# The first two blocks of rows multiplied with raw tokens, and the norm and the shift applied to the sums

## The chip, the cores and the metric

The kernel runs on one core of a Trainium2 chip. The metric is the device time of one execution in microseconds. A core has TensorE (PE in the profile, its weight loads PEld), VectorE (DVE), ScalarE (ACT), GpSimd (POOL) and SyncE (SP), which run side by side and wait for one another by semaphores. SBUF is the memory that they work from, PSUM the one that PE writes its sums to, and DMAs bring data from HBM.

## The reference

One layer of a block for 512 latent tokens of width 2048, with 256 context tokens. What matters here is its beginning:

```
shift, scale, gate = jnp.split(silu(c) @ w_ada + b_ada, 3)
h = rmsnorm(x, norm_g) * (1 + scale) + shift
p = h @ w_in                                # 512 x 2048 by 2048 x 9216
q, k, v, z_a, u_b, z_b, g_a, g_b = columns of p
attn = attention(rope(rmsnorm(q)), [k, kc], [v, vc])
y = (sig(g_a) * ((attn * silu(z_a)) @ w_pa)
     + sig(g_b) * ((fourier(u_b) * silu(z_b)) @ w_pb)) @ w_o
out = rmsnorm(x + gate * y, final_g)
```

`rmsnorm(x, g)` is x times a factor per token, 1/sqrt(mean(x^2) + eps), times g. So a row of h is, for input channel k and token t, x[k,t] * gain[k] * r[t] + shift[k], where gain is norm_g * (1 + scale). All is float32.

## The kernel before

The tokens lie transposed in SBUF: `xt` holds 16 blocks of 128 channels by 512 tokens. A block of rows of h (512 tokens, 128 channels) is made from `xt`, the gain and shift of its channels and the factor `rx` of each token (`make_h`, lines 378 to 383), and split in two parts, `hh` (rounded to fp32r) and `hl` (what is left). Weights are split likewise into `whi` and `wlo` (`split_from`, lines 119 to 121: ACT rounds, DVE subtracts). A product of float32 accuracy is then three products on PE (`mm3`, lines 219 to 223).

The start has these parts, in the program's order:

- The token loads (`XCH`, lines 64 and 336), then the modulation matrix of block 0 (two loads of 1 MB, `wada_load`), three start pieces of the weights, and the matrix of block 1 (lines 373 to 376), all on SP's queue. From block 2 on, the matrix comes by POOL's queue into four buffers.
- `squares` (lines 351 to 371): the tokens' squares by ACT, three of 16 by DVE, pairs added by DVE, and eight products on PE with a matrix of ones, which sum over the channels and leave the sum of each token on all partitions; root and reciprocal give `rx`.
- `modulation` of a block (lines 447 to 455): silu(c) times its part of the matrix (32 PE instructions, line 391), a copy by ACT, two transposes (line 401), and three small DVE operations that give shift and gain. For block 0, some products with ones that nothing uses keep PE at work (`warm`, line 411).
- The loop over blocks (lines 464 to 476): modulation, rows, then as many of the start's products as are owed.

`start_work` (lines 413 to 445) is a generator of these products: for each group of blocks (`GROUPS`, line 40) ten column tiles of 128 (four for the Fourier branch, four for its gate, two for heads of q) whose sums are added up over the groups in `part` and `q01` (`pt`, `keep`), and four tiles of V (`vals`). Its PSUM sums come from a ring of four banks (`bank`). A group of one block has 10 x 3 + 4 x 3 = 42 products of 128 x 128 by 512 columns. The weights of a piece are loaded ahead into four raw buffers on SP's queue (`start_load`, `load_more`) and split three pieces ahead (`get`). The loads wait for the buffers.

Each engine works through its instructions in a fixed order. The programming layer sets it when the kernel is built: by the order of the program, but an instruction whose inputs are estimated to be late lets later ones pass.

## Time and profile before

| | us |
|---|---|
| median of 3 runs | 1391.73 |
| lowest and highest | 1391.26, 1393.59 |
| the profiled execution | 1392.62 |
| its span, first to last instruction | 1390.8 |
| PE busy, share of the span | 1358.8, 98% |
| DVE busy | 890.4, 64% |
| ACT busy | 617.8, 44% |

The profile is of one execution. A row of its groups or of its timeline names the line, the engine, the operation and the tile that is written from those that are read, with shapes as partitions by elements. A group's row ends with its count, its busy time in us, the mean of one in ns, and, behind the bar, how long the engine had stood idle before and for whom. In the timeline a row starts with start and length in us from the first instruction, and shows in brackets an idle time before it. In the chain of waits a row is start, length and what the chain ran through there. A matmul's length in the profile is longer than its distance to the next, since they overlap; the distance is what counts.

### The profile page before, as it was taken

How to read it: one execution, taken by the hardware profiler on the slowest of the kernel's cores; microseconds unless marked ns; L12 is line 12 of the kernel's file. 1: busy time of each engine (PE TensorE's matmuls, PEld its weight loads, DVE VectorE, ACT ScalarE, POOL GpSimd, SP SyncE). 2: the span in 40 equal slices, each digit the busy share in tenths (PEclk: the TensorE clock that was granted, in tenths of full speed). 3: DMA queues.
4: the chain of work that ended last, by engine and by line, in shares of the span. 5: the costliest groups of instructions: out<-in, count | busy, mean ns of one | idle time of the engine just before them, and what ended most of it. 6: DMA issues, size and time to landing. Idle time of an engine off the chain costs nothing.

```text
span 1390.8 us, 17626 instructions
## 1 busy us (share of the span) xinstructions
PE 1358.8 (98%) x6858; PEld 1113.7 (80%) x6858; DVE 890.4 (64%) x1172; ACT 617.8 (44%) x849; POOL 106.6 (8%) x161
## 2 busy tenths in 40 slices
PE   7999999999999999999999899999999999999996
PEld 4667789888888888888888688888888888888874
DVE  5765596867866668666644776665856544437767
ACT  5322253534545544544544645444544322233534
POOL 0110000011100001000001100000010100000100
PEclk9999999999999999999999999999999999999998
DMA  9897453545543435434447998988898844244883
GB/s 384 328 349 264 159 185 107 185 123 184 162 140 107 128 112 160 139 99 121 135 131 275 312 285 239 259 227 257 266 269 301 327 151 137 76 137 153 182 224 136
DMA packets 73812, 275.29 MB, mean 198 GB/s; under 512 B 8448, under 2 KB 9088, under 8 KB 69376
## 3 DMA queue, kind: packets, MB, share of 16 engines
q1 hardware_dynamic: 52272, 183.18, 39.8%
q0 software_dynamic: 16272, 73.42, 18.7%
q10 hardware_dynamic: 5184, 17.57, 3.3%
q8 instruction: 54, 0.88, 0.3%
q14 instruction: 30, 0.25, 0.1%
HBM read 248.95 MB, written 25.17 MB: 197 GB/s over the span
## 4 chain that ended last, share of the span: by engine, by line
PE 89%; DMA 5%; DVE 4%; ACT 1%; issue 1%; DVEq 0%; SPq 0%; ACTq 0%
PE pb L221 12%; PE pb L222 12%; PE pb L223 12%; PE x L222 7%; PE x L223 7%; PE x L221 6%; PE y L222 6%; PE y L223 6%; PE y L221 6%; PE pd L221 3%; PE pd L223 3%; PE pd L222 3%; PE pd L930 2%; PE pd L391 2%; DMA wr<-in_w_g 2%; DVE wlo L121 1%
## 5 line engine op out<-in xcount | busy, mean ns | idle before, releaser
L120 ACT ACTIVATE whi<-wr 128x1024 fp32r<-128x1024 f32 x188 | 195.7, 1045 | 336.5 <-PE y L223 89.5
L121 DVE TENSOR_TENSOR wlo<-wr,whi 128x1024 fp32r<-128x1024 f32 x188 | 225.8, 1204 | 170.9 <-ACT whi L120 170.5
L221 PE MATMUL pb<-hh,whi 128*128 128x512 f32 x512 | 206.7, 405 | 1.3 <-ACT hh L381 1.3
L222 PE MATMUL pb<-hl,whi 128*128 128x512 f32 x512 | 200.7, 392 | 0.1
L223 PE MATMUL pb<-hh,wlo 128*128 128x512 f32 x512 | 200.4, 392 | 0.0
L222 PE MATMUL y<-wlo,s 128*128 128x512 f32 x348 | 137.1, 394 | 7.1 <-DVE wlo L121 7.1
L221 PE MATMUL y<-whi,s 128*128 128x512 f32 x348 | 136.6, 393 | 0.6 <-ACT whi L120 0.6
L223 PE MATMUL y<-whi,s 128*128 128x512 f32 x348 | 136.3, 392 | 0.0
L221 PEld LDWEIGHTS pb<-hh,whi 128*128 128x128 f32 x512 | 96.1, 188 | 22.5 <-issue 3.7
L223 PEld LDWEIGHTS pb<-hh,wlo 128*128 128x128 f32 x512 | 96.1, 188 | 21.0 <-issue 0.4
L222 PEld LDWEIGHTS pb<-hl,whi 128*128 128x128 f32 x512 | 96.4, 188 | 17.1 <-DVE hl L382 1.0
L222 PE MATMUL x<-wlo,s 128*128 128x512 f32 x248 | 97.0, 391 | 0.6 <-DVE wlo L121 0.6
L221 PE MATMUL x<-whi,s 128*128 128x512 f32 x248 | 97.0, 391 | 0.0
L223 PE MATMUL x<-whi,s 128*128 128x512 f32 x248 | 96.8, 390 | 0.0
L120 ACT ACTIVATE whi<-R 128x1024 fp32r<-128x1024 f32 x57 | 60.0, 1058 | 55.7 <-PE x L223 38.0
L222 PEld LDWEIGHTS y<-wlo,s 128*128 128x128 f32 x348 | 65.6, 189 | 23.3 <-DVE wlo L121 9.8
L121 DVE TENSOR_TENSOR wlo<-R,whi 128x1024 fp32r<-128x1024 f32 x57 | 69.0, 1220 | 20.4 <-ACT whi L120 20.4
L921 ACT ACTIVATE p<-pd,mx 128x768 f32<-128x768 f32 x48 | 43.2, 900 | 84.5 <-DVE mx L919 84.5
L221 PEld LDWEIGHTS y<-whi,s 128*128 128x128 f32 x348 | 65.8, 189 | 14.8 <-ACT whi L120 1.0
L223 PEld LDWEIGHTS y<-whi,s 128*128 128x128 f32 x348 | 65.8, 189 | 13.6
L121 DVE TENSOR_TENSOR ptl<-pd,pth 128x768 fp32r<-128x768 f32 x48 | 45.8, 953 | 33.0 <-ACT pth L120 33.0
L221 PE MATMUL pb<-whi,hh 128*128 128x512 f32 x144 | 57.1, 397 | 0.0
(283 smaller groups left out, 2705.1 us busy)
## 6 DMA issues: line engine op xcount, KB each, us to landing
wr<-in_w_g SPq DMA_DIRECT2D x80, 512.0 KB, 8.0
wa<-in_w_ss POOLq DMA_DIRECT2D x28, 1024.0 KB, 8.5
wr<-in_w_m SPq DMA_DIRECT2D x44, 512.0 KB, 3.7
wr<-in_w_gate SPq DMA_DIRECT2D x32, 512.0 KB, 3.7
wr<-in_w_pab SPq DMA_DIRECT2D x32, 512.0 KB, 5.2
R<-in_w_g POOLq DMA_DIRECT2D x32, 512.0 KB, 10.1
wr<-in_w_o SPq DMA_DIRECT2D x32, 512.0 KB, 4.1
wr<-in_w_start SPq DMA_DIRECT2D x26, 512.0 KB, 7.1
```

The costliest lines, as they stand in the source:

```text
L120: nc.scalar.activation(hi, src, ACT.Copy)
L121: nc.vector.tensor_tensor(lo, src, hi.bitcast(F32), op=ALU.subtract)
L221: nc.tensor.matmul(o, ah, bh, start=start, stop=False, skip_group_check=cont)
L222: nc.tensor.matmul(o, ah, bl, start=False, stop=False, skip_group_check=cont)
L223: nc.tensor.matmul(o, al, bh, start=False, stop=stop, skip_group_check=cont)
L391: nc.tensor.matmul(acc[32 * j : 32 * j + 32, :256], c2[:, kk, :], w[:, k, :], start=kk < 4, stop=kk >= KK - 4)
L921: nc.scalar.activation(p, sc[:, :NKEY], ACT.Exp, bias=mx[:, 0:1], accum_out=mx[:, 1:2])
L930: nc.tensor.transpose(tp[:, k * P : (k + 1) * P], p[:, k * P : (k + 1) * P], ident)
```

## The change

Block by block, h @ w is sum over k of (x * gain * r + shift) * w. For the first two blocks the change multiplies x * gain (`make_early`) instead of the rows of h, sums as before, and adds w's product with the shift (`sft`, two equal columns; its sums are gathered in `sv`). When `rx` is there the ten sums of 128 x 512 are multiplied by it on DVE, and the shift's sums are added with the next group (`keep`). V's tiles have tokens on the partitions; for them the true rows of the two blocks are made later, and the two blocks' V pieces become one. The order of loads on SP is: matrix of block 0, tokens of block 0, two start pieces, matrix of block 1, tokens of block 1, two start pieces, the other tokens. The norm is computed after the two blocks' modulation: squares are added on DVE into one running sum, and PE sums them per token with the squares as weights (`token_norm`), so that the root and the reciprocal work on four columns; a diagonal matrix and one product with ones bring the factors back to all partitions. It stands in the program after 45 of the 60 products of the two blocks.

```diff
--- before.py
+++ after.py
@@ -38,6 +38,8 @@
 NS = len(START)
 
 GROUPS = [(0, 1), (1, 1), (2, 2), (4, 4), (8, 4), (12, 4)]
+
+EARLY = 2
 RAW = 4
 
 HL, MORE_HL = 3, 2
@@ -61,7 +63,7 @@
     f = {"P1": "Z5", "P2": "S2", "Q6": "S3", "P7": "S4"}.get(name)
     return [(f, pc - 1)] if f and g == 0 and pc in (1, 2) else []
 
-XCH = [(0, 2), (2, 2), (4, 4), (8, 4), (12, 2), (14, 2)]
+XCH = [(0, 1), (1, 1), (2, 2), (4, 4), (8, 4), (12, 2), (14, 2)]
 
 
 def start_pieces():
@@ -71,7 +73,10 @@
     for kb, nk in GROUPS:
         per = 8 // nk
         new = [(kb, nk, t, min(per, NS - t)) for t in range(0, NS, per)]
-        new += [(kb + i, min(2, nk), -1, 4) for i in range(0, nk, 2)]
+        if kb + nk == EARLY:
+            new.append((0, EARLY, -1, 4))
+        elif kb >= EARLY:
+            new += [(kb + i, min(2, nk), -1, 4) for i in range(0, nk, 2)]
         for p in new:
             cols = p[1] * p[3] * P
             r.append((off, cols) + p)
@@ -333,47 +338,49 @@
         (nc.gpsimd if kb > 1 else nc.sync).dma_start(w, w_ss[kb, :, 8 * h : 8 * h + 8, :])
         return w
 
-    for a, n in XCH:
+    def x_load(i):
+        a, n = XCH[i]
         nc.sync.dma_start(xt[:, a : a + n, :], xT[:, a : a + n, :])
+
+    wada = {(0, h): wada_load(0, h) for h in range(2)}
+    x_load(0)
+    for _ in range(2):
+        start_load()
+    wada.update({(1, h): wada_load(1, h) for h in range(2)})
+    x_load(1)
+    for _ in range(2):
+        start_load()
+    for i in range(2, len(XCH)):
+        x_load(i)
 
 
     c2 = pap.tile([P, KK, 32], F32, name="c2")
     nc.vector.memset(c2, 0.0)
     rt = pap.tile([P, 1], F32, name="rt")
+    ex = pap.tile([P, 2 * KK], F32, name="ex")
     ce = pap.tile([P, 2 * KK], F32, name="ce")
-    nc.scalar.activation(ce, cvt, ACT.Exp, scale=-1.0)
-    nc.scalar.activation(rt, ce[:, 0:1], ACT.Sqrt)
-    nc.vector.tensor_scalar(ce, ce, 1.0, None, op0=ALU.add)
+    nc.scalar.activation(ex, cvt, ACT.Exp, scale=-1.0)
+    nc.scalar.activation(rt, ex[:, 0:1], ACT.Sqrt)
+    nc.vector.tensor_scalar(ce, ex, 1.0, None, op0=ALU.add)
     nc.vector.reciprocal(ce, ce)
     nc.vector.tensor_tensor(c2[:, :, 0:2].rearrange("p k j -> p j k"),
                             cvt.rearrange("p (j k) -> p j k", j=2),
                             ce.rearrange("p (j k) -> p j k", j=2), op=ALU.mult)
-    def squares(srcs, n, r, new, run=None):
+    def squares(srcs, n, r, new, run):
 
         acc = bank2()
         for q in range(0, KK, 2):
             a, b = new(), new()
             for t, src in zip((a, b), srcs(q)):
-                if run is None and t is b and q in (4, 8, 10):
-                    nc.vector.tensor_tensor(t, src, src, op=ALU.mult)
-                else:
-                    nc.scalar.activation(t, src, ACT.Square)
+                nc.scalar.activation(t, src, ACT.Square)
             nc.vector.tensor_tensor(a, a, b, op=ALU.add)
-            if run is None:
-                nc.tensor.matmul(acc[:, :n], ones, a, start=q == 0, stop=q == KK - 2)
-            elif q == 0:
+            if q == 0:
                 nc.vector.tensor_copy(run, a)
             else:
                 nc.vector.tensor_tensor(run, run, a, op=ALU.add)
-        if run is not None:
-            nc.tensor.matmul(acc[:, :n], ones, run, start=True, stop=True)
+        nc.tensor.matmul(acc[:, :n], ones, run, start=True, stop=True)
         nc.scalar.activation(r, acc[:, :n], ACT.Sqrt, bias=eps_t[:, 0:1], scale=1.0 / D)
         nc.vector.reciprocal(r, r)
-
-    wada = {(0, h): wada_load(0, h) for h in range(2)}
-    while todo and len(ahead) < 3:
-        start_load()
-    wada.update({(1, h): wada_load(1, h) for h in range(2)})
 
     def make_h(hi, lo, src, rr, kb, j, pool, n):
         tmp = pool.tile([P, n], F32, tag="htmp", bufs=2, name=uid("ht"))
@@ -414,13 +421,15 @@
         ends = {kb + nk for kb, nk in GROUPS}
         begins = {kb for kb, nk in GROUPS}
 
-        def keep(dst, acc, first):
+        def keep(dst, acc, first, add=None):
             if first:
                 nc.scalar.copy(dst, acc)
+            elif add is not None:
+                nc.vector.scalar_tensor_tensor(dst, acc, add, dst, op0=ALU.add, op1=ALU.add)
             else:
                 nc.vector.tensor_tensor(dst, acc, dst, op=ALU.add)
 
-        vacc = None
+        vacc, sacc = None, None
         for p in start_pieces():
             kb, nk, t, nt = p[2:]
             wh, wl = get(("start", p))
@@ -429,9 +438,22 @@
                     acc = bank()
                     c = slice(P * i, P * i + P)
                     for k in range(nk):
-                        mm3(acc, wh[:, k, c], wl[:, k, c], hhi[kb + k], hlo[kb + k], k == 0, k == nk - 1)
-                    keep(pt(t + i), acc, kb == 0)
+                        r = early[kb] if kb < EARLY else (hhi[kb + k], hlo[kb + k])
+                        mm3(acc, wh[:, k, c], wl[:, k, c], r[0], r[1], k == 0, k == nk - 1)
+                    keep(pt(t + i), acc, kb == 0, sv[:, t + i, 0:1] if kb == EARLY else None)
                     yield 3 * nk
+                if kb < EARLY:
+
+                    if t == 0:
+                        sacc = bank()[:, : 2 * NS].rearrange("p (n v) -> p n v", v=2)
+                    for i in range(nt):
+                        c = slice(P * i, P * i + P)
+                        mm3(sacc[:, t + i, :], wh[:, 0, c], wl[:, 0, c], sft[kb][0], sft[kb][1], True, True)
+                    if t + nt == NS:
+                        if kb == 0:
+                            nc.vector.tensor_copy(sv, sacc)
+                        else:
+                            nc.vector.tensor_tensor(sv, sv, sacc, op=ALU.add)
             else:
                 if kb in begins:
                     vacc = [bank() for _ in range(4)]
@@ -454,20 +476,89 @@
         nc.vector.tensor_scalar(gain[:, kb, :], sp[:, 1, :], bsc1[:, kb : kb + 1], ng[:, kb : kb + 1],
                                 op0=ALU.add, op1=ALU.mult)
 
+    early, sft = [], []
+    sv = pap.tile([P, NS, 2], F32, name="sv")
+
+    def make_early(kb):
+
+        u = hm.tile([P, 2, T], F32R, tag="h", name=uid("u"))
+        nc.scalar.activation(u[:, 0, :], xt[:, kb, :], ACT.Copy, scale=gain[:, kb, 0:1])
+        nc.vector.scalar_tensor_tensor(u[:, 1, :], xt[:, kb, :], gain[:, kb, 0:1], u[:, 0, :].bitcast(F32),
+                                       op0=ALU.mult, op1=ALU.subtract)
+        early.append((u[:, 0, :], u[:, 1, :]))
+        st = pap.tile([P, 2, 2], F32R, tag="sft", bufs=EARLY, name=uid("sft"))
+        nc.vector.tensor_copy(st[:, 0, :], shift[:, kb, :])
+        nc.vector.tensor_tensor(st[:, 1, :], shift[:, kb, :], st[:, 0, :].bitcast(F32), op=ALU.subtract)
+        sft.append((st[:, 0, :], st[:, 1, :]))
+
+    def sum_squares(run):
+
+        for q in range(0, KK, 2):
+            sq = hm.tile([P, 2, T], F32, tag="h", name=uid("sq"))
+            nc.scalar.activation(sq[:, 0, :], xt[:, q, :], ACT.Square)
+            if q < KK - 2:
+                nc.scalar.activation(sq[:, 1, :], xt[:, q + 1, :], ACT.Square)
+            else:
+                nc.vector.tensor_tensor(sq[:, 1, :], xt[:, q + 1, :], xt[:, q + 1, :], op=ALU.mult)
+            if q == 0:
+                nc.vector.tensor_tensor(run, sq[:, 0, :], sq[:, 1, :], op=ALU.add)
+            else:
+                nc.vector.tensor_tensor(sq[:, 0, :], sq[:, 0, :], sq[:, 1, :], op=ALU.add)
+                if q < KK - 2:
+                    nc.vector.tensor_tensor(run, run, sq[:, 0, :], op=ALU.add)
+        return sq[:, 0, :]
+
+    def token_norm(rx, parts, diag):
+
+        acc = bank()
+        for t in range(4):
+            for i, a in enumerate(parts):
+                nc.tensor.matmul(acc[:, 2 * t : 2 * t + 2], a[:, t * P : t * P + P], ones[:, 0:2],
+                                 start=i == 0, stop=i == len(parts) - 1)
+        r = pap.tile([P, 4, 2], F32, name="rcol")
+        nc.scalar.activation(r, acc[:, 0:8].rearrange("p (t v) -> p t v", v=2), ACT.Sqrt, bias=eps_t[:, 0:1], scale=1.0 / D)
+        nc.vector.reciprocal(r, r)
+        d = diag.rearrange("p (t c) -> p t c", t=4)
+        nc.vector.tensor_tensor(d, ident[:, None, :].broadcast_to([P, 4, P]), r[:, :, 0:1].broadcast_to([P, 4, P]), op=ALU.mult)
+        acc = bank()
+        nc.tensor.matmul(acc, ones, diag, start=True, stop=True)
+        nc.scalar.copy(rx, acc)
+
     wacc = bank()
     rx = pap.tile([P, T], F32, name="rx")
-    squares(lambda q: (xt[:, q, :], xt[:, q + 1, :]), T, rx, lambda: hm.tile([P, 2, T], F32, tag="h", name=uid("sq"))[:, 0, :])
-    modulation(0)
-
     work = start_work()
     done = 0
-    for kb in range(KK):
-        if kb:
-            modulation(kb)
+
+    def do(n):
+        d = 0
+        while d < n:
+            d += next(work)
+        return d
+
+    for kb in range(EARLY):
+        modulation(kb)
+        make_early(kb)
+    scratch = hm.tile([P, 2, T], F32, tag="h", name="run")
+    last_two = sum_squares(scratch[:, 0, :])
+    done += do(30)
+    done += do(15)
+    token_norm(rx, (scratch[:, 0, :], last_two), scratch[:, 1, :])
+    done += do(15)
+
+    def make_rows(kb):
         if kb % 2 == 0:
             pairs.append([hm.tile([P, 2, T], F32R, tag="h", name=uid(n)) for n in ("hh", "hl")])
         hhi[kb], hlo[kb] = (t[:, kb % 2, :] for t in pairs[-1])
         make_h(hhi[kb], hlo[kb], xt[:, kb, :], rx, kb, 0, pap, T)
+
+    for kb in range(EARLY):
+        make_rows(kb)
+    for kb in range(EARLY, KK):
+        modulation(kb)
+        make_rows(kb)
+        if kb == EARLY:
+            for i in range(NS):
+                nc.vector.tensor_tensor(pt(i), pt(i), rx, op=ALU.mult)
 
         full = max([k + n for k, n in GROUPS if k + n <= kb] or [0])
         owed = 42 * full
```

## The prediction

> **What bounds the kernel now.** I read the profile's page first, then busy time by stretches, then the chain of waits and the timelines of the start, where the change lies. From the page:
>
> ```profile
> span 1390.8 us, 17626 instructions
> PE 1358.8 (98%) x6858; PEld 1113.7 (80%) x6858; DVE 890.4 (64%) x1172; ACT 617.8 (44%) x849; POOL 106.6 (8%) x161
> PE 89%; DMA 5%; DVE 4%; ACT 1%; issue 1%; DVEq 0%; SPq 0%; ACTq 0%
> ```
>
> TensorE is busy for 98% of the span and carries 89% of the chain that ended last. For the stretch of the start (its bounds and length, then busy time and instructions of PE, PEld, DVE, ACT, POOL, then the granted clock, the DMA share and GB/s):
>
> ```profile
> 26.74:174.00 147.26, 147.09 (x978) 106.10 (x979) 88.13 (x146) 45.28 (x66) 13.24 (x25) 1.00 0.75 282
> ```
>
> From 26.74 us on PE has no hole in this stage: 147.09 busy of 147.26. So whatever PE work is added behind the first product costs its full length, and whatever moves the first product forward gains its full length, unless it opens a hole. Later loads wait for free buffers and so move along with the work; a shift at the start should reach the end. How the first product comes to stand at 26.74, in the chain of waits (start, length, what):
>
> ```profile
> 1.16 4.03 DMA xt<-in_xT
> ...
> 8.65 10.04 PE pd L363 x16
> 18.72 0.70 ACT rx L370
> 19.44 0.75 DVE rx L371
> ```
>
> All of the tokens, their squares and the norm stand in line before any product. The same on PE's timeline, with the first block's modulation behind the squares:
>
> ```profile
> 18.61 1.93 PE L391 MATMUL pd<-wa,c 128*32 128x256 f32 x32
> 20.47 1.56 PE L411 MATMUL pb<-wa,ones 128*128 128x256 f32 x6
> 21.87 0.38 PE L401 MATMUL pd<-ident,ado 128*128 128x128 f32 x2
> 22.09 2.32 PE L411 MATMUL pb<-ado,ones 128*128 128x256 f32 x10
> 24.34 1.07 PE L391 MATMUL pd<-wa,c 128*32 128x256 f32 x16
> 26.74 0.73 PE L221 MATMUL pb<-hh,whi 128*128 128x512 f32 x2 [1.32 <-ACT hh L381]
> ...
> 29.56 1.07 PE L391 MATMUL pd<-wa,c 128*32 128x256 f32 x16
> ...
> 52.02 0.39 PE L222 MATMUL pb<-wlo,hh 128*128 128x512 f32 x1
> 52.25 0.40 PE L223 MATMUL pb<-whi,hl 128*128 128x512 f32 x1
> ...
> 56.31 0.50 PE L221 MATMUL pb<-hh,whi 128*128 128x512 f32 x1
> ```
>
> A product takes 0.23 us from start to start (52.02 to 52.25). At 56.31 the third block's products begin; the 84 of the first two blocks and five modulations are done. After that point both kernels have the same PE work, so I compare when each reaches it.
>
> **The change, part by part.** *The earlier first product.* The first block's modulation now needs 2 MB of its matrix, which go out first.
>
> ```profile
> 10.00:20.00 10.00, 10.00 (x43) 4.08 (x45) 5.79 (x10) 4.76 (x9) 0.00 (x0) 1.00 1.01 419
> wa<-in_w_ss POOLq DMA_DIRECT2D x28, 1024.0 KB, 8.5
> 20.03 0.70 POOL L333 DMA_DIRECT2D wa<-in_w_ss  x1 [18.73 <-PE pd L391]
> ```
>
> At 419 GB/s 1 MB takes 2.5 us. The first 512 KB of tokens were issued at 1.16 and used at 5.2, so a first 1 MB lands at about 6.4 and the second at 8.9. On SP's queue the token loads move behind it, and the two blocks' start pieces become four loads, their V columns one load later. The first half of the matrix product runs on arrival; the second is 16 instructions, 0.7 us at the cadence of 18.61 to 20.16. But PE has then just woken. What that means is in the weight loads of the squares:
>
> ```profile
> 13.93 0.34 PEld L363 LDWEIGHTS pd<-sq,ones 128*128 128x128 f32 x1 [0.52 <-issue]
> 14.65 0.19 PEld L363 LDWEIGHTS pd<-sq,ones 128*128 128x128 f32 x1 [0.39 <-DVE sq L361]
> 15.08 0.19 PEld L363 LDWEIGHTS pd<-sq,ones 128*128 128x128 f32 x1 [0.24 <-issue]
> ```
>
> A load takes 0.34 up to 13.93 and 0.19 from 14.65, and from there they come 0.43 apart; all 16 took 10.04, not 16 x 0.43 = 6.9. So PE runs at about half speed for 6.0 us after its first instruction at 8.65, though the granted clock reads 1.00. Before, the squares bore this; now the first block's modulation does. So: matrix product to 10.6 (1.4 at half speed, and the gap), three warming multiplications at 2.8 instead of 1.4 to 13.5, transposes to 13.9. Behind the transposes DVE makes the gain, here for the second block:
>
> ```profile
> 31.87 0.17 DVE L405 TENSOR_REDUCE adr<-pd 128x4 f32<-128x16 f32 x1 [4.40 <-PE pd L401]
> 32.08 0.23 DVE L453 TENSOR_SCALAR shift<-adr,small 128x2 f32<-128x2 f32 x1
> 32.21 0.28 DVE L454 TENSOR_SCALAR gain<-adr,bsc,small 128x2 f32<-128x2 f32 x1
> ```
>
> From 31.87 to the end at 32.49 are 0.6; with 0.3 from PE to DVE, 0.1 to ACT and 0.7 for ACT's copy of a row (as rx at 18.72) the first row is ready at 15.6. Five warming multiplications stand ahead on PE: 0.43 apiece per instruction until about 14.65, then 0.22, which ends at 16.4. That is my first product; 15.0 if the speed doubles by 12, 18.2 if the half speed lasts through. Gain 26.74 - 16.4 = 10.3 us. The Trainium skill, page "TensorE: Matmul & The Clock Gate", section "What's actually happening", says that the clock lets half its pulses through until one free-running window of 3.4 us was busy. Its windows would end between 12.3 and 15.7 here, an estimated first product between 15.3 and 17.0 and a sum between +0.2 and +1.9; the trace's 6.0 us agrees with it.
>
> *Work that PE had done before its first product and now does behind it.* The first half of the second block's modulation (24.34, 1.07 us): +1.0. The eight squares' products on PE (10.04 us) go away, but they lay before the first product and are in the 10.3.
>
> *The shift's columns.* For each of two blocks, ten column tiles by three products: 60 multiplications of two columns, each with its own 128 x 128 weights. No row shows one. The nearest:
>
> ```profile
> L391 PEld LDWEIGHTS pd<-wa,c 128*32 128x32 f32 x512 | 15.5, 109 | 15.4 <-issue 4.6 <-PE pb L222 2.1 <-DMA wa<-in_w_ss 0.4
> L222 PEld LDWEIGHTS pb<-hl,whi 128*128 128x128 f32 x160 | 30.1, 188 | 6.8 <-DVE hl L382 1.0 <-issue 0.4
> L401 PE MATMUL pd<-ident,ado 128*128 128x128 f32 x32 | 6.2, 275 | 0.1
> ```
>
> Loading 32 columns of weights shows 109 ns, loading 128 shows 188: 96 more columns are 79 ns, so 128 would take some 105, and the transposes, with 128 x 128 weights, come 0.11 apart (two from 21.87 take 0.38, of which 0.27 is one alone). I take 0.12 us: 7.2 in all. Ends: 0.05 as in the modulation's rows (1.55 us over 31 steps), 3.0 in all; or a full product's 0.23, 13.8. The Trainium skill, same page, section "LDWEIGHTS (loading the stationary operand)", has the loading time go with the columns, an estimated 107 ns here, 6.4 in all, which would bring the sum below to +0.5. Its section "Back-to-back issue gap" lists about 25 ns for moving widths of 1 to 64, an estimated 1.5 in all and a sum of -4.4; this is the faster rival below.
>
> *The norm by columns.* Eight two-column products with float weights, two instructions each, 16 x 0.12 = 1.9; one 128 x 512 product with ones, two instructions of 0.43, 0.86; two changes between kinds of work at about 0.3. Together +3.4 (2.0 to 5).
>
> Sum at the third block: -10.3 + 1.0 + 7.2 + 3.4 = +1.3 us.
>
> *What lies beside PE.* These are the rows:
>
> ```profile
> L361 DVE TENSOR_TENSOR sq<-sq,sq 128x512 f32<-128x512 f32 x8 | 5.3, 687 | 0.7 <-ACT sq L360 0.6
> L371 DVE RECIPROCAL rx<-rx 128x512 f32<-128x512 f32 x1 | 3.4, 3354 | 3.7 <-ACT rx L370 3.7
> L421 DVE TENSOR_TENSOR vals<-pb,vals 128x512 f32<-128x512 f32 x3 | 1.9, 676 | 0.0
> L382 DVE SCALAR_TENSOR_TENSOR hl<-ht,shift,hh 128x512 fp32r<-128x512 f32 x3 | 2.2, 748 | 1.8 <-ACT hh L381 1.8
> L360 ACT ACTIVATE sq<-xt 128x512 f32<-128x512 f32 x13 | 7.4, 619 | 3.5 <-DMA xt<-in_xT 3.3
> L419 ACT COPY part<-pb 128x512 f32<-128x512 f32 x8 | 4.5, 588 | 2.4 <-PE pb L223 2.2
> ```
>
> DVE loses 11 operations of the squares (7.6), the wide reciprocal (3.4) and four additions to V (2.7), 13.7; it gains 15 operations of 0.69 for the squares (10.3), two of 0.75 for the early rows, small ones for the shift and the norm (2.3), the diagonal (0.7) and ten scalings of the sums (6.9), 21.7. ACT keeps about its squares (15 x 0.62 for 13) and gains two copies.
>
> When is the norm there? SP's queue carries 9.25 MB up to the last token rows (4 tokens, 4 modulation, 1.25 start pieces). The first 2 land by 8.9; from there POOL's queue issues the next blocks' matrices as soon as a buffer is free, as at 20.03, and 1 MB of it in the median 8.5 us is 29% of the rate, so SP's MB takes 3.5 us and the tokens end at 34.6 (27.0 without POOL). Then square and sum 1.4, column products 1.9, root, reciprocal and diagonal 1.3, product with ones 0.86, copy 0.6 and handovers 0.4: norm at 41, first true rows 1.5 later, 42.6. PE comes to the V columns, which need them, at 16.4 + modulations (two halves of 1.07 and a whole of 1.93, 4.1) + 60 products (13.7) + 7.2 + 3.4 = 44.8. That covers it by 2.2 us. DVE then has six operations for rows (4.5), the scalings (6.9), the fourth block's rows (1.5) and two gains (1.2), 14.1, ready at 55; PE is at the third block at 56.31 + 1.3 = 57.6. Both fit, but queues are strict in order and a small loss is likely: between nothing and the 6.9 of the scalings I take 1.0, near the lower end because of the spare time. The forecast is +2.3. The profiled execution took 1392.62 (span 1390.8), 0.9 above the median of 1391.73; 1394.9 against its own time, 1394.0 against the median.
>
> **The rivals.** *The norm comes too late (slower).* Place: V's products on PE, behind the last token rows. It decides when these land after 36.8 (34.6 plus the 2.2 spare), or when the queue of ACT holds squares that wait for tokens ahead of the copies that free PSUM (0.59 each, while one bank of four is held by the shift's sums). For it: the tokens go behind 4 MB of the matrix, and DMA shows 1.01 of its capacity at 10 to 20. Against: the 60 products and the columns as cover. Price: 4 us (the column products take their place after 45 of the 60 products, so the last 15, 3.4, and some wait stand open). +6.3, 1398.0.
>
> *It does not start as early as it should (slower).* The order of instructions on PE is fixed beforehand; if the second block's modulation is put ahead of the first products, PE waits for its second MB, which lands at 8.9 + 2.9 MB x 3.5 = 19.1 rather than 16.4. The rows at 24.34 and 29.56 speak against: there products of the first block were put between the halves. Price 2.7: +5.0, 1396.7.
>
> *The shift's columns cost next to nothing (faster).* If two-column products run at the 0.05 of the modulation's rows, 4.2 us come off, and with the quicker clock 1.4 more: -1.9 to -3.3, 1389.8 to 1388.4. Against: those rows load 32 columns of weights, not 128.
>
> **How the numbers follow.** About 0.2% (2.8 us) is what a measurement of this kernel can tell from no change. Forecast 0.46 (of this 0.34 within 0.2% and 0.12 above, as 1394.5 is the bound), late norm 0.20, late start 0.12 (0.02 within), cheap columns 0.22 (0.16 beyond 0.2%). So faster 0.16, same 0.42, slower 0.42. The likeliest case alone spans 1392 to 1397. The range from 1389.0 to 1399.5 takes in the late norm and most of the cheap columns and leaves out the dear columns (13.8) and the quickest clock.
>
> **What would show it.** Right: first product at 15 to 18; sixty two-column products some 0.12 apart; PE dense from there; third block at 57 to 60 against 56.31. Wrong: a hole on PE at V or at the norm's columns; a modulation between 16 and 20 waiting on its load; columns at 0.05 or 0.2; or order changes behind the start, which I cannot see beforehand, of more than 2 us.

## The result: 1% slower, and the profile after

The changed kernel takes 1406.9 us (median, 1405.4 to 1407.5) against 1391.5 for the kernel before (1390.3 to 1393.6) on the same chip: a ratio of 1.0104 with an interval of 1.0092 to 1.0116, or about 15.4 us more by the medians. The forecast was 1394.0 with a range up to 1399.5. Slower had been given 0.42, as much as no change; the size was missed by far.

The profiled execution of the changed kernel took 1405.35 us. These are the lines of its page that answer to the three of before:

```profile
span 1403.6 us, 17771 instructions
PE 1369.3 (98%) x6920; PEld 1124.9 (80%) x6920; DVE 895.9 (64%) x1190; ACT 619.3 (44%) x853; POOL 106.7 (8%) x161
PE 79%; DMA 8%; issue 6%; DVE 4%; ACT 1%; POOL 0%; SPq 0%; DVEq 0%; POOLq 0%; ACTq 0%
```

TensorE is still busy for 98%, but it carries 79% of the chain in place of 89%; DMA and "issue" have taken the share. The share of busy time hides the loss, because an instruction at half the clock counts as busy too. Now busy time by stretches. The start of the stage is the first product, its end the first product of the next stage, which takes the tokens' context; the kernel before reaches that point at 219.58 us, the changed one at 234.12. The stretches of the changed kernel begin at 14.57, 0.4 us behind its first product. First before, then after (bounds and length, then busy time and instructions of PE, PEld, DVE, ACT and POOL, granted clock, DMA share, GB/s):

```profile
26.74:219.58 192.84, 192.67 (x1191) 144.27 (x1192) 126.84 (x213) 69.21 (x106) 13.24 (x25) 1.00 0.70 255
```

```profile
14.57:234.12 219.55, 212.76 (x1284) 158.16 (x1283) 143.71 (x244) 79.90 (x125) 13.76 (x26) 0.96 0.67 247
14.57:37.50 22.93, 21.55 (x147) 13.82 (x145) 9.31 (x20) 12.43 (x23) 1.73 (x4) 0.93 1.02 416
37.50:53.00 15.50, 10.62 (x60) 6.62 (x61) 10.09 (x21) 5.55 (x11) 1.45 (x3) 0.72 0.97 392
53.00:62.00 9.00, 9.00 (x46) 7.91 (x45) 4.75 (x7) 2.33 (x4) 0.00 (x0) 0.73 0.01 3
62.00:234.12 172.12, 171.59 (x1034) 129.82 (x1033) 119.56 (x198) 59.60 (x89) 10.58 (x20) 1.00 0.63 224
```

The holes and the missing clock lie ahead of 62 us. PE stands idle for 6.8 us between its first product and the marker (219.55 less 212.76), 4.9 of them between 37.5 and 53; before it had 0.17. And the granted clock, 1.00 throughout before, is 0.93, 0.72 and 0.73 in the three stretches: 1.6 + 4.3 + 2.4, some 8.4 us of full clock missing, a part of it inside the holes. Behind 62 us PE is as dense as before. The marker stands 14.5 us later; the profiled executions are 12.7 apart, so 1.8 is given back in later stages.

PE's timeline shows where (start, length, what, and in brackets the idle time ahead of it and who ended it):

```profile
9.14 1.48 PE L398 MATMUL pd<-wa,c 128*32 128x256 f32 x16 [0.49 <-DMA wa<-in_w_ss]
10.56 1.56 PE L418 MATMUL pb<-wa,ones 128*128 128x256 f32 x6
...
14.15 1.05 PE L226 MATMUL pb<-u,whi 128*128 128x512 f32 x3
...
16.11 1.07 PE L398 MATMUL pd<-wa,c 128*32 128x256 f32 x16
...
22.93 0.25 PE L228 MATMUL pb<-sft,wlo 128*128 128x2 f32 x1
23.04 0.25 PE L226 MATMUL pb<-sft,whi 128*128 128x2 f32 x1
...
26.82 2.53 PE L398 MATMUL pd<-wa,c 128*32 128x256 f32 x18
29.77 0.79 PE L226 MATMUL pb<-u,whi 128*128 128x512 f32 x1 [0.42 <-ACT part L426]
...
37.90 1.91 PE L398 MATMUL pd<-wa,c 128*32 128x256 f32 x26
42.01 0.44 PE L408 MATMUL pd<-ident,ado 128*128 128x128 f32 x2 [2.21 <-ACT ado L405]
44.45 0.59 PE L516 MATMUL pb<-ones,run 128*128 128x2 f32 x2 [2.00 <-DVE run L508]
...
47.63 0.57 PE L516 MATMUL pb<-ones,sq 128*128 128x2 f32 x2
48.83 1.92 PE L398 MATMUL pd<-wa,c 128*32 128x256 f32 x10 [0.63 <-DVE adr L412]
50.68 2.08 PE L524 MATMUL pb<-run,ones 128*128 128x512 f32 x2
...
52.98 0.63 PE L227 MATMUL pb<-u,whi 128*128 128x512 f32 x1
53.41 0.63 PE L228 MATMUL pb<-u,wlo 128*128 128x512 f32 x1
```

The first product comes at 14.15, 12.6 us earlier than before. The run of the first block's columns (22.79 to 25.4) costs 0.11 us each. One tile and six more columns later, the modulation at 26.82 takes 2.53 us for 18 instructions (16 take 1.07 at 16.11), and the rows from 44.45 to 52.98 are at half speed (a full product steps in 0.43 from 52.98 to 53.41, instead of 0.23). Between 42.45 and 44.45 PE waits for DVE's running sum of the squares. And 15 full products with 30 columns of the second block still stand behind the norm, in an order fixed beforehand, although their operands had been there since 34.4 us.

Why was the sum late? POOL's, ACT's and DVE's timelines:

```profile
8.99 0.70 POOL L338 DMA_DIRECT2D wa<-in_w_ss  x1 [7.70 <-PE pd L398]
...
28.84 0.53 POOL L338 DMA_DIRECT2D wa<-in_w_ss  x1 [7.32 <-PE pd L398]
```

```profile
38.48 0.63 ACT L498 ACTIVATE sq<-xt 128x512 f32<-128x512 f32 x1 [1.01 <-DMA xt<-in_xT]
```

```profile
29.43 0.68 DVE L504 TENSOR_TENSOR run<-sq 128x512 f32<-128x512 f32 x1
...
44.32 0.68 DVE L506 TENSOR_TENSOR sq<-sq 128x512 f32<-128x512 f32 x1
```

POOL sent five 1 MB loads between 8.99 and 28.84, and all five had landed by 38.1; counted from the end of the first issue that is 5.2 MB in 28.5 us, 184 GB/s of some 416. The tokens behind SP's queue landed at 41.0, not 34.6. ACT got the square of the ninth part at 38.48, and the fifteen operations that the squares cost DVE, spread from 29.43 on by its waits for them, ended at 45.0.

### The profile page after: what moved, and what is told of

Read it like the earlier page. It is cut to its first block, busy times and chain, and to the rows that moved or that the text cites. A ratio compares the mean times of both kernels' runs of the same rounds, so it can differ in the third digit from the quotient of the medians.

```text
span 1403.6 us, 17771 instructions
## 1 busy us (share of the span) xinstructions
PE 1369.3 (98%) x6920; PEld 1124.9 (80%) x6920; DVE 895.9 (64%) x1190; ACT 619.3 (44%) x853; POOL 106.7 (8%) x161
## 4 chain that ended last, share of the span: by engine, by line
PE 79%; DMA 8%; issue 6%; DVE 4%; ACT 1%; POOL 0%; SPq 0%; DVEq 0%; POOLq 0%; ACTq 0%
PE pb L226 11%; PE pb L227 10%; PE pb L228 10%; PE x L227 6%; PE x L226 6%; PE x L228 6%; PE y L227 5%; PE y L228 5%; PE y L226 5%; DMA wr<-in_w_g 3%; PE pd L226 3%; PE pd L228 3%; PE pd L227 3%; DMA xt<-in_xT 2%; PE pd L398 2%
## 5 line engine op out<-in xcount | busy, mean ns | idle before, releaser
L125 ACT ACTIVATE whi<-wr 128x1024 fp32r<-128x1024 f32 (+1 forms) x187 | 195.3, 1049 | 344.1 <-PE pb L227 93.3
L126 DVE TENSOR_TENSOR wlo<-wr,whi 128x1024 fp32r<-128x1024 f32 (+1 forms) x187 | 225.5, 1210 | 176.5 <-ACT whi L125 175.6
L226 PE MATMUL pb<-hh,whi 128*128 128x512 f32 x492 | 198.6, 404 | 0.0
L227 PE MATMUL pb<-hl,whi 128*128 128x512 f32 x492 | 192.3, 391 | 0.0
L228 PE MATMUL pb<-hh,wlo 128*128 128x512 f32 x492 | 192.2, 391 | 0.0
L228 PEld LDWEIGHTS pb<-hh,wlo 128*128 128x128 f32 x492 | 92.4, 188 | 20.1
L226 PEld LDWEIGHTS pb<-hh,whi 128*128 128x128 f32 x492 | 92.4, 188 | 18.8 <-issue 2.9
L227 PEld LDWEIGHTS pb<-hl,whi 128*128 128x128 f32 x492 | 92.7, 188 | 15.7 <-DVE ht L387 0.4
L126 DVE TENSOR_TENSOR ptl<-pd,pth 128x768 fp32r<-128x768 f32 x48 | 45.7, 953 | 30.5 <-ACT pth L125 30.3
## 6 DMA issues: line engine op xcount, KB each, us to landing
R<-in_w_g POOLq DMA_DIRECT2D x32, 512.0 KB, 10.2
```

Source lines behind the costliest of these rows:

```text
L125: nc.scalar.activation(hi, src, ACT.Copy)
L126: nc.vector.tensor_tensor(lo, src, hi.bitcast(F32), op=ALU.subtract)
L226: nc.tensor.matmul(o, ah, bh, start=start, stop=False, skip_group_check=cont)
L227: nc.tensor.matmul(o, ah, bl, start=False, stop=False, skip_group_check=cont)
L228: nc.tensor.matmul(o, al, bh, start=False, stop=stop, skip_group_check=cont)
```

## The experiments

Five theories were set against each other. (The clock is the granted TensorE clock; a column is one of the two-column products with the shift.) T: the tokens are late, because POOL's loads take their rate. C: the columns' PE work is the loss. O: the fixed order, with the norm ahead of 15 products. N: a run of narrow two-column products pulls the clock down to half. D: only PE's waits pull it down. Later ones ask what the norm by columns costs by itself. Ratios are against the kernel before on the same chip (medians there 1389.7 for the first four, 1390.4 for the next four, 1390.5 for the last three). The runs were made on different chips, so the excess over the kernel before is what can be compared; the change has 15.4 us, with 1.0092 to 1.0116 for its ratio.

**Matrices behind the tokens.** The loads of blocks 2 and 3 go to SP's queue, behind the tokens.

```diff
-        (nc.gpsimd if kb > 1 else nc.sync).dma_start(w, ...
+        (nc.gpsimd if kb > 3 else nc.sync).dma_start(w, ...
```

> The matrices of blocks 2 and 3 go out on SP's queue behind the tokens, not on POOL's beside them; nothing else is changed. Theory T (tokens late: in the changed kernel they land until 41.0 us because POOL's queue carries five 1 MB loads meanwhile, so the norm is late, PE runs out of work and falls to half speed): tokens land by 30, the norm's column products start near 33 instead of 44.5, no stretch with a granted clock under 0.9, time 1393 to 1396. Theory C (the extra work on PE, columns and norm, is the loss): unchanged, 1405 to 1407. Theory O (the fixed order, which puts the norm's columns ahead of the last 15 products, is the loss): about 1402 to 1406, since that order stays.

Measured: 1406.1 us, ratio 1.0117 (1.009 to 1.0143), an excess of 16.4: not better than the change itself. The tokens were there at 28.5, 12.5 us earlier, as T said; but the norm's columns moved only from 44.45 to 38.96. From the stretches and the waits of this kernel:

```profile
30.00:40.00 10.00, 4.04 (x16) 3.14 (x14) 10.00 (x18) 4.80 (x9) 0.00 (x0) 0.84 1.03 424
40.00:50.00 10.00, 8.61 (x34) 6.85 (x33) 5.38 (x9) 1.58 (x3) 0.00 (x0) 0.59 0.24 89
```

```profile
PE pb L516 <- DVE run L508: 6.0, 1, 6.0
```

DVE is busy for all of 30 to 40: its operations for the squares, among its other work, fill that time, the running sum is ready at 38.8, and PE waits 6.0 us for it. With the transfers out of the way, DVE holds PE in their place. And the clock is at half from 38.0 to 48.2 all the same.

**Without the columns.** Zeros stand in their place, so the shift of the first two blocks is missing from ten tiles.

```diff
-                    for i in range(nt):
-                        ...
-                        mm3(sacc[:, t + i, :], wh[:, 0, c], wl[:, 0, c], sft[kb][0], sft[kb][1], True, True)
...
+                        nc.vector.memset(sv, 0.0)
```

> The 60 two-column products with the shift are left out (zeros are added in their place, so the shift of the first two blocks is missing from ten tiles of the output's path). Theory T: they lie partly where PE waits for the norm anyway, 3 to 5 us less, 1402 to 1404. Theory C: 7 to 10 us less, 1397 to 1400. Theory O: 3 to 6 us less.

Measured: 1402.5, ratio 1.0085 (1.0068 to 1.0103), an excess of 12.7, 2.7 us less than the change; the intervals overlap. The 6.8 us of columns were worth less than their length: a part of them had covered the wait, which is longer now, and in this trace PE also came to its full clock later (first product at 16.05).

```profile
40.00:50.00 10.00, 3.56 (x15) 3.08 (x15) 4.59 (x8) 2.93 (x6) 0.00 (x0) 0.58 1.02 416
```

There is no half clock at 27 now (1.00 from 14.3 to 41.6), as N wanted, but a long one from 41.6 on (0.50 up to 58.7), which begins in a wait of PE of 5.3 us. So C is at most a third of the loss.

**Tokens first.** All token loads ahead of the modulation's matrices, the rest as changed.

```diff
+    for i in range(len(XCH)):
+        x_load(i)
     wada = {(0, h): wada_load(0, h) for h in range(2)}
-    x_load(0)
     ...
```

> All tokens are loaded first again, then the matrix of block 0, two start pieces, the matrix of block 1; the early products, the columns and the norm by columns stay. Theory T: tokens land by 14, the norm is ready before it is needed, no half speed after the start; the first product comes at 24 to 27 as before the change, and the columns (7) and the second block's modulation come on top: 1396 to 1400. Theory C: no gain, 1405 to 1408, because the extra work is all still there. Theory O: 1400 to 1406.

Measured: 1412.3, ratio 1.016 (1.0142 to 1.0178). A miss: the first product comes at 28.4 and nothing pays for it, since the norm's columns wait behind 45 products and the columns until 54.0. It shows one thing plainly, on PE's timeline:

```profile
38.40 0.25 PE L228 MATMUL pb<-sft,wlo 128*128 128x2 f32 x1
...
41.65 0.35 PE L226 MATMUL pb<-sft,whi 128*128 128x2 f32 x1
41.87 0.35 PE L227 MATMUL pb<-sft,whi 128*128 128x2 f32 x1
```

A run of 30 columns begins at 38.16 with a step of 0.11, and from 40.7 its step is 0.21, while PE waits for nothing. PE's last waits before it were 0.18 us at 38.0 and 1.1 at 34.9. That speaks for N against D.

**The norm last.** The norm's columns and its product with ones go behind all 60 early products.

```diff
-    token_norm(rx, (scratch[:, 0, :], last_two), scratch[:, 1, :])
     done += do(15)
+    token_norm(rx, (scratch[:, 0, :], last_two), scratch[:, 1, :])
```

> The norm stands in the program behind all 60 products of the first two blocks, not behind 45. Theory T: the tokens still land at 41, but 15 products and 30 column products fill PE's holes ahead of the norm and run at full speed: 4 to 6 us less, 1401 to 1403. Theory O: the whole loss goes, 1392 to 1396. Theory C: unchanged, 1405 to 1408.

Measured: 1403.6, ratio 1.0105 (1.0088 to 1.0122), an excess of 13.9; that cannot be told from the change. The wait at the norm is gone, and others stand in its place:

```profile
PE pb L226 <- DVE part L430: 3.8, 1, 3.8
PE pb L226 <- ACT part L426: 2.2, 1, 2.2
```

PE comes to sums whose PSUM banks are not free, because DVE adds squares and ACT waits with squares for tokens ahead of the copies. O is at most a small part.

**Columns between the products.** In the program each tile's three columns stand right behind that tile's three products, instead of 24 and 6 in a row.

```diff
+                    if kb < EARLY:
+                        ...
+                        mm3(sacc[:, t + i, :], wh[:, 0, c], wl[:, 0, c], sft[kb][0], sft[kb][1], True, True)
                     yield 3 * nk
```

> The 60 column products are issued each behind the wide products of its own tile instead of 24 and 6 in a row; the same instructions. Theory N (a run of two-column products looks idle to the clock gate and drops PE to half speed; in the changed kernel the clock falls at 27.1 and 57.8, each time 3 to 5 us into or behind such a run): no half speed between 20 and 32, 1 to 3 us less, 1403 to 1406 beside 1406.9. Theory D (only PE's waits for the norm drop the clock): clock and time unchanged.

Measured: 1403.3, ratio 1.0092 (1.0076 to 1.0109), an excess of 12.9, 2.5 less than the change; the intervals overlap. The half clock at 27 is gone (1.00 in the stretch from 20 to 30, where the change has 0.86); the waits stay, and so does the half clock behind them. The edit did only half of what it was meant to do: in the order in which the kernel was built, the first block's columns stand between the products, but 26 of the second block's still stand in a row from 33.65 on, behind a wait of 2.0 us and at 0.21 us each.

**Both.** Interleaved columns, and the matrices behind the tokens.

```diff
+        (nc.gpsimd if kb > 3 else nc.sync).dma_start(w, ...
...
+                        mm3(sacc[:, t + i, :], wh[:, 0, c], wl[:, 0, c], sft[kb][0], sft[kb][1], True, True)
                     yield 3 * nk
```

> The columns between the products, and the matrices of blocks 2 and 3 behind the tokens on SP's queue. Theory N with T: no half speed before the norm's wait; tokens by 29; DVE's chain of squares then sets the norm near 37 to 39, so one hole of some 4 us and one stretch of half speed stay: 1398 to 1403. Theory D: as with the loads alone, about 1406.

Measured: 1402.9, ratio 1.0088 (1.0073 to 1.0104): no better than the interleaving alone. PE still waits 4.5 us for DVE's sum, from 37.9 on. And here too 26 columns stand in a row, from 28.43 to 32.04. PE had waited for no more than 0.3 us since its first product, and yet the step of the columns goes from 0.11 to 0.21 at 30.4:

```profile
30.40:37.20 6.80, 6.80 (x23) 5.93 (x24) 2.86 (x5) 5.59 (x11) 0.00 (x0) 0.50 1.02 420
```

So this run speaks for N once more, and what is left in it is the norm's path and a run of columns.

**The norm by columns alone.** The kernel before, with only its norm exchanged: running sum on DVE, columns, diagonal, product with ones.

```diff
-    squares(lambda q: (xt[:, q, :], xt[:, q + 1, :]), T, rx, ...)
+    scratch = hm.tile([P, 2, T], F32, tag="h", name="run")
+    last_two = sum_squares(scratch[:, 0, :])
+    token_norm(rx, (scratch[:, 0, :], last_two), scratch[:, 1, :])
```

> The kernel before with the norm by columns alone: DVE adds all the squares, PE sums them per token, root and reciprocal on four columns, diagonal and ones bring them back. No early products, no other order of loads. If the norm by columns is a saving in itself: first product before 26.7 and 1385 to 1390. My expectation from the rows: 15 additions in one chain on DVE end near 18, columns at half speed until 21, the factors on all partitions at 25 where they were at 22.8: first product 2 to 5 us later, 1392 to 1396.

Measured: 1398.3, ratio 1.0045 (1.0028 to 1.0062). This part of the change alone costs 7.9 us. Its PE timeline:

```profile
17.92 0.59 PE L479 MATMUL pb<-ones,run 128*128 128x2 f32 x2 [17.92 <-DVE run L471]
...
21.10 0.57 PE L479 MATMUL pb<-ones,sq 128*128 128x2 f32 x2
21.60 1.91 PE L391 MATMUL pd<-wa,c 128*32 128x256 f32 x10
23.44 2.08 PE L487 MATMUL pb<-run,ones 128*128 128x512 f32 x2
25.45 2.15 PE L391 MATMUL pd<-wa,c 128*32 128x256 f32 x22
...
33.05 0.96 PE L221 MATMUL pb<-hh,whi 128*128 128x512 f32 x3 [0.59 <-ACT hh L381]
```

In the kernel before, PE multiplied the sums of two squares with ones as they came (8.65 to 18.7), while tokens were still loaded and squared, and from 14.65 on it was at full speed. Here it stands still until 17.92, starts at half speed, and does the norm's columns, a part of the modulation and the product with ones at half speed until 26.8. The first product moves from 26.74 to 33.05, 6.3 us.

**The old norm back.** As "both", but with the eight products with ones on PE and the wide reciprocal.

```diff
-    last_two = sum_squares(scratch[:, 0, :])
+    old_squares(lambda q: (xt[:, q, :], xt[:, q + 1, :]), T, rx, ...)
     done += do(30)
     done += do(15)
-    token_norm(rx, (scratch[:, 0, :], last_two), scratch[:, 1, :])
```

> As the run with both, but the norm as before the change: pairs of squares added by DVE, eight products with ones on PE, root and wide reciprocal. Early products and columns stay. If DVE's chain of squares is what makes the norm late once the tokens are in time: PE has no hole before it and no half speed after 20, the eight products add 6.9 and the norm's columns 3.4 fall away: 1393 to 1398. If not: 1402 or more.

Measured: 1399.4, ratio 1.0059 (1.004 to 1.0078), 3.5 less than "both" on the same chip; its profiled execution is the fastest of its six, 1394.7, with a span of 1393.0. In that one the clock is full from 10.5 us to 778; the longest run of columns in its built order is 18, from 31.05 to 32.98. Since "both" has a run of 26, the 3.5 us are not the norm's alone. The six spread over 8 us at nearly the same mean clock (0.994 to 0.996); why is open.

**The old norm, columns in a row.** The same, with the columns in runs again: one edit against the last kernel.

```diff
                     yield 3 * nk
+                if kb < EARLY:
+                    ...
+                    for i in range(nt):
+                        mm3(sacc[:, t + i, :], wh[:, 0, c], wl[:, 0, c], sft[kb][0], sft[kb][1], True, True)
```

> As the run with the old norm (tokens ahead of the matrices of blocks 2 and 3, products with ones for the norm), whose profile kept the full clock from 10.5 us on; only the columns stand in a run of 24 and 6 behind their pieces again. Theory N (a run of narrow products drops the clock without any wait of PE): half speed 4 to 6 us after the start of a run of columns, near 27 and again near 40, 2 to 5 us more in the profiled span (1393.0 there), 1395 to 1399 for it. Theory D (only waits drop it): full clock, same span within 1.

Measured: 1401.3, ratio 1.0078 (1.006 to 1.0096); the profiled execution took 1399.1 against 1394.7. The times of the two kernels overlap, so what the place of the columns costs is not settled by them; the mean clock of a whole execution is 0.988 to 0.993 in this one's four and 0.994 to 0.996 in the other's six. The stretches, first with interleaved columns, then in runs:

```profile
20.00:30.00 10.00, 10.00 (x61) 7.01 (x61) 5.19 (x12) 8.07 (x16) 0.00 (x0) 1.00 0.98 386
30.00:40.00 10.00, 10.00 (x47) 6.97 (x46) 9.12 (x14) 5.32 (x10) 0.00 (x0) 1.00 1.02 424
40.00:50.00 10.00, 7.93 (x59) 4.86 (x57) 8.81 (x11) 3.88 (x6) 1.25 (x2) 1.00 0.43 156
```

```profile
20.00:30.00 10.00, 10.00 (x65) 7.40 (x57) 5.72 (x13) 8.09 (x16) 0.00 (x0) 0.87 1.01 409
30.00:40.00 10.00, 10.00 (x33) 5.86 (x31) 7.67 (x13) 4.67 (x8) 0.00 (x0) 0.96 1.02 420
40.00:50.00 10.00, 10.00 (x54) 7.63 (x53) 7.67 (x7) 1.75 (x2) 0.00 (x0) 0.72 0.45 145
```

PE is busy for all 30 us in the second kernel, and yet its clock falls to 0.87, 0.96 and 0.72; in the first it stays at 1.00, though PE idles for 2.1 us of the last ten. The edit moves nothing but the columns: runs of 24 and 6 here, of 18 at most there. D falls as the sole cause, and N is shown for runs of 24 and more.

**The old norm without columns.** As the old norm, with zeros in place of the columns.

```diff
-                        mm3(sacc[:, t + i, :], wh[:, 0, c], wl[:, 0, c], sft[kb][0], sft[kb][1], True, True)
...
+                        nc.vector.memset(sv, 0.0)
```

> As the run with the old norm, without the 60 columns (zeros stand in their place, so the shift of the first two blocks is missing). If the columns cost what their rows show (5.8 us there) and nothing waits behind them: 5 to 7 us less, a profiled span of 1386 to 1388 and 1391 to 1395 by median. If DVE or the norm's rows are what PE then waits for: 0 to 3 less.

Measured: 1395.7, ratio 1.0033 (1.0021 to 1.0045), an excess of 5.2, where the kernel with interleaved columns has 9.0.

```profile
40.00:50.00 10.00, 5.37 (x42) 3.41 (x41) 10.00 (x16) 2.66 (x4) 1.25 (x2) 0.81 0.89 344
```

DVE is busy for all of 40 to 50 and PE for half of it. So even with no columns, full clock up to 46 and the tokens in time, PE runs into DVE, which has the squares, the wide reciprocal and the true rows to do in one stretch. The account of this kernel closes to 0.5 us: first product 11.7 us earlier (15.0), the norm's products with ones now behind it 5.1, the half modulation 1.0, holes of 4.6 and 1.2, and 6.8 us at half clock, at most 3.4; that makes +3.6, and its marker stands 4.1 later than before. What stood ahead of the first product for nothing stands behind it at its full price.

**One early block.** Only the first block is multiplied early, with the old norm, interleaved columns and all tokens ahead of the later matrices.

```diff
-EARLY = 2
+EARLY = 1
```

> Early products for the first block alone, columns between them, old norm, all tokens ahead of the matrices of blocks 1 to 3. From the rows: the first product stays near 14.5 (12 less than 26.7), 30 columns cost 3.3, the eight products with ones 6.9 now lie behind the first product, half a modulation 1.0: the sum is -1, tokens by 21 and the norm near 28 where PE has work until 28. 1388 to 1393 if the ten scalings on DVE (6.9) hide behind V and two modulations, 1394 to 1398 if they do not.

Measured: 1397.9, ratio 1.0056 (1.0042 to 1.0069). Half the columns and half the early products:

```profile
30.00:40.00 10.00, 8.66 (x69) 5.53 (x72) 8.40 (x12) 6.86 (x13) 0.00 (x0) 1.00 0.41 153
40.00:50.00 10.00, 7.50 (x52) 3.83 (x44) 9.97 (x20) 2.68 (x5) 1.25 (x2) 1.00 0.92 337
50.00:60.00 10.00, 9.50 (x64) 5.79 (x68) 9.64 (x14) 2.76 (x5) 1.06 (x2) 1.00 0.83 304
```

Full clock throughout, and still PE has 4.3 us of holes while DVE is full or nearly so. No version of the early start that was run reaches the kernel before.

## Why the prediction was wrong

*The earlier first product* came out better than forecast: 14.15 instead of 16.4, below the quickest end of 15.0. PE started at 6.7 and had its full speed from 10.0, not from 14.65 (by the steps of its rows; the granted clock reads 1.00 there as it does in the kernel before). I had read 6.0 us of half speed off the squares of the kernel before. The Trainium skill, page "TensorE: Matmul & The Clock Gate", section "What's actually happening", has 3.4 us of a busy PE suffice; here it was 3.3. But that was luck. Nine of the experiments start with the same instructions on PE, and their traces have the first product at 14.0 to 16.1. In the kernel without the columns half speed lasts until 14.3, 8 us behind PE's start at 6.4, and the six warming multiplications take 2.93 us where the change has 1.56:

```profile
10.67 2.93 PE L418 MATMUL pb<-wa,ones 128*128 128x256 f32 x6
...
16.05 0.82 PE L226 MATMUL pb<-u,whi 128*128 128x512 f32 x2
```

So the forecast's 16.4 lies near the slow end of what came, and 3.4 us cannot be counted on. The gain in this trace is 12.6 us, 2.3 more than in the sum.

*The half modulation* stands at 16.11 as 1.07 us, where the sum has 1.0.

*The shift's columns*: 60 at 0.113 us, 6.8 in place of 7.2. The term was right as PE work, and the rival that priced them at next to nothing did not come. But a run of them also takes the clock down, which no term of the sum held.

*The norm by columns* was mis-sized at +3.4 (2.0 to 5). As PE instructions the term is about right at full speed (16 x 0.113 and two of 0.43 are 2.7), but I let the eight old products go for nothing, as work that "lay before the first product". They had a second effect: they brought PE to full speed while the tokens came in. By itself the exchange costs 7.9 us on the kernel before; inside the change, taking it back was worth 3.5 at most (with the other repairs in place, and with a shorter run of columns). The step counted instructions and not what the removed ones kept running.

*The time of the norm* is the step that decided. Forecast: tokens at 34.6, norm at 41, V reached at 44.8, 2.2 to spare. Measured: tokens at 41.0, columns of the norm at 44.45, its copy rx ready at 53.4. Three sizes failed in it. The first is the rate: I gave POOL 29% of it, "1 MB in the median 8.5 us", and it took 44%, because the modulations of the first two blocks, now ahead of the norm, freed buffers at 9.0, 12.4, 17.5 and 21.0 us, so that POOL had two loads under way for most of the time. The Trainium skill, page "DMA: Bandwidth & Descriptors", section "Queues, rings and completion order", says that each DMA engine goes round robin between the queues that have work; half each, an estimated 210 GB/s, and the 184 here agree with that better than with my 29%. The second is DVE: I counted the squares as two operations behind the last tokens (1.4 us), while 15 operations of 0.69 us take 10 us, and DVE has other work between them. With the tokens there at 28.5 the sum was ready at 38.8 only. The first without the second gains nothing (an excess of 16.4 against 15.4). The third is the path from the columns to rx: 5.1 us in the forecast, 9.0 measured (44.45 to 53.4), since all of it ran at half clock. Of the norm's 12.4 us of delay the tokens are 6.4, DVE some 2.0 and the half clock 3.9.

*The rival "the norm comes too late"* named the place, the condition (tokens after 36.8) and the 15 products left open. Its price of 4 us held the wait alone. Holes cost 6.8 us, and the half clock, behind waits and behind runs of columns, costs again: some 8.4 us of clock are missing up to 62 us. Together with 1.0, 6.8 and some 2.7 for the norm's PE work they come to 25.7 at most, since holes and half clock overlap in part; the marker's +14.5 and the gain of 12.6 ask for 27.1, so 1.4 us or a little more are not accounted for.

*The DVE scalings*, which I put at 1.0 of their 6.9: in the change itself they show little, since PE is as late as they are: they end at 72.3, not by 55, and the third block's products begin at 74.98, where I had 57.6 (one more modulation lies ahead of them than before). When the rest is mended PE stands idle beside a full DVE: with one early block even at full clock.

The late start because of the second modulation didn't occur: the half at 16.11 did not wait (its load landed at 14.2), and products stood between the halves.

What stays open: the 8 us of spread with the old norm, of which the varying half speed at the start might explain some 2 (not shown), and the 1.4 us above.

## What to carry to other kernels

Work that an engine did ahead of the critical products (here wide products on PE during the token loads) may be what brings its clock up: before replacing it by "cheaper" instructions, ask what the engine will be doing in that time, and at which clock the next work then starts. A hole on TensorE can cost its length and again the half clock behind it, so 2 us of spare time are no cover where the order is fixed and the wait hangs on two DMA queues and on a chain of another engine. Narrow products belong between wide ones, not in a run of 24 or more; and whether they stand there is read from the built order in the trace, not from the program.

## What the runs showed of the hardware

- A run of two-column products, each with its own 128 x 128 weights, brings the granted clock to 0.5 though PE has no wait: 24 in 2.6 us, one tile, and 6 more ahead of 27.4 in the kernel with the columns in a row; from the 24th of 30 on in the kernel with the tokens first; from 30.4 in a run of 26 that began at 28.43 in "both". The same 60 in runs of at most 18 between full products do not (old norm, 1.00 from 10.5 us on).
- Such a product steps in 0.11 us at full clock and 0.21 at half: the rate of its weights, not of its two columns (a product of the modulation, 256 columns wide but with 32 columns of weights, steps in 0.05). The Trainium skill, page "TensorE: Matmul & The Clock Gate", section "LDWEIGHTS (loading the stationary operand)", gives an estimated 107 ns for 128 columns, which agrees.
- The stretches of half clock between 20 and 70 us last 3.4, 6.8 or 10.2 us (27.1 to 30.5, 44.2 to 54.4 and 57.8 to 61.2 in the change), and 17.1 us in the kernel without the columns (41.6 to 58.7). Two holes of 2.2 and 2.0 us, with two transposes between them, were followed by 10.2 us at half clock, in which the narrow norm columns ran.
- PE's half speed after its first instruction lasts 3.3 us in the change and 8 us in the kernel without the columns, with the same instructions at the start.
- Two queues that both have loads waiting share the rate about evenly: 184 of 416 GB/s for POOL's, whose 1 MB loads took 8.9 to 9.6 us each with two under way.
